# High-part products first, and four gate tiles inside the last attention steps, in a hybrid decoder step

## The chip, the cores and the metric

One core of a Trainium2 chip runs the whole layer. The metric is the device time of one execution in microseconds; before the change the median of three executions is 2021.8 us (2020.32 to 2022.55).

## The reference

One decoder layer (width 2048) is applied to 288 tokens: 32 of eight decode requests, 256 of a prompt. All matrix products use shared float32 weights:

```
xn   = rmsnorm(x)
proj = xn @ w_in            # r, k, v, three small low-rank inputs, q, k, v of attention, gate_a, gate_b
y_a  = rwkv_branch(...)     # token shift, decay, delta-rule state scan, group norm, output gate
y_b  = swa(q, k, v)         # window attention, ALiBi, sinks
mix  = sigmoid(gate_a) * y_a + sigmoid(gate_b) * y_b
h    = x + mix @ w_out
h    = h + relu(rmsnorm(h) @ w_up)^2 @ w_down
y    = rmsnorm(h)
```

Caches and states are returned as well.

## The kernel before

Activations lie transposed: a channel tile has 128 partitions and 288 token columns. Every float32 operand of a large product is split into a high part (rounded to fp32r) and a low part (the rest), and the product is the sum of three: high weight by high activation, high by low, low by high.

**A half tile.** Weights arrive as half tiles of 128 x 1024 (eight blocks of the contraction). `weights` (L152) issues the load of one on SP's queue (L158, four buffers `raw`), ScalarE casts it to `whi` (L146) and VectorE subtracts to get `wlo` (L147); `whi` and `wlo` have two buffers each. `dense` (L164) takes two half tiles for one output tile (one for a half of the output projection). For each of the eight blocks k it issues three matmuls in a row: L177 (`whi`, high activation), L178 (`whi`, low activation), L179 (`wlo`, high activation). So the third matmul of a half tile already needs `wlo`. A dense call accumulates into one of two PSUM banks `mm`; the bank comes free when its result is read out.

**Phase 1** first makes four small tiles while x arrives (L296 to L316; the same three products, L314 to L316, for four tiles and two blocks at a time in four PSUM banks). Then a loop goes over 16 channel tiles (`pair`: k, v and r tiles and their scan operands). Between its parts run steps of the attention generator (`attention`, by a pacing list) and of the side generators: `chain` (the state scan of two channel tiles) and `finish` (output gate, gate tile `ga`, merge, store to `mixd` in DRAM). After the loop come the remaining attention steps, which are the twelve of its last group, each followed by `advance`, three side steps (L403, L404). Then the attention's SBUF pools are closed (L405, L406), and in their place come `h`, `mhi`, `mlo` (L409 to L412) and a pool `late`. The first eight merged tiles are loaded back from DRAM to `h` (L414) and split (L416); the last four gate tiles (channel tiles 12 to 15, `ga12` to `ga15`) are computed (L422) and their tanh is kept in the tiles `tgl` of the pool `late` (L424). The output projection's first half follows (L430, 16 half tiles on `mhi`/`mlo`), then in phase 2 its second half and the MLP, all by `dense`.

**What sets the order.** The program is traced in this order, and a planner then orders each engine's instructions by a simulated timeline; an instruction that is ready may be put ahead of earlier ones that are not. On the chip each engine and SP's queue take their instructions in the planned order. A tile in reused SBUF waits for the last reader of what lay there before.

Of the kernel before, what the change touches and what calls it, by code (L numbers as in the profile page):

```python
# [8 lines left out]
F32 = mybir.dt.float32  # L9
F32R = mybir.dt.float32r  # L10
AF = mybir.ActivationFunctionType
# [6 lines left out]
KT = D // 128  # L18
# [111 lines left out]
class Builder:  # L130
# [33 lines left out]
    def dense(self, src, x, kts=range(KT), pre=None, m=128):  # L164


        nc = self.nc
        ps = self.ps_mm.tile([128, 512], F32, name="mm")
        if m < 128:
            nc.vector.memset(ps[m:128, :NT], 0.0)  # L170
        for i, kt in enumerate(kts):
            if i % 8 == 0:
                whi, wlo = pre[i // 8] if pre else self.weights(src[i // 8])
            k = i % 8
            a, b = whi[:, k * 128:k * 128 + m], wlo[:, k * 128:k * 128 + m]
            hi, lo = x(kt)
            nc.tensor.matmul(ps[:m, :NT], lhsT=a, rhs=hi, start=(i == 0), stop=False)  # L177
            nc.tensor.matmul(ps[:m, :NT], lhsT=a, rhs=lo, start=False, stop=False)  # L178
            nc.tensor.matmul(ps[:m, :NT], lhsT=b, rhs=hi, start=False, stop=(i == len(kts) - 1))  # L179
        return ps[:, :NT]  # L180

    def xin(self, kt):
# [60 lines left out]
    def phase1(self, c1, ph):  # L243
# [16 lines left out]
        with ExitStack() as st:  # L260
            xp = self.pool("xin", 1, ctx=st)
            x = xp.tile([128, KT, NT], F32, name="x")
            shi = xp.tile([128, KT, NT], F32R, name="shi")
            slo = xp.tile([128, KT, NT], F32R, name="slo")
            rstd = xp.tile([128, NT], F32, name="rstd")
            acc = xp.tile([128, 2, NT], F32, name="acc")
            pss = self.ps_lo.tile([128, 512], F32, name="lo")

            win4 = io["win"][TIX["dw"]:TIX["dw"] + 4].rearrange("t a p (k c) -> a p t k c", k=8)
            pz = [pool.tile([128, 512], F32, name=n)[:, :NT] for pool, n in ((self.ps_gr, "gr"), (self.ps_gr, "gr"), (self.ps_ch, "ch"), (self.ps_ch, "ch"))]  # L270

            def arrive(q):
                two = slice(2 * q, 2 * q + 2)
                for kt in (2 * q, 2 * q + 1):
                    w = v["norm_mix_w"][:, kt:kt + 1]
                    if kt % 2:
                        nc.vector.tensor_scalar(out=shi[:, kt, :], in0=x[:, kt, :], scalar1=w, scalar2=None, op0=ALU.mult)
                    else:
                        nc.scalar.activation(out=shi[:, kt, :], in_=x[:, kt, :], func=AF.Copy, scale=w)
                    nc.vector.scalar_tensor_tensor(out=slo[:, kt, :], in0=x[:, kt, :], scalar=w, in1=shi[:, kt, :], op0=ALU.mult, op1=ALU.subtract)  # L280

                sq = acc if q == 2 else xp.tile([128, 2, NT], F32, name="xsq", bufs=2)
                nc.scalar.activation(out=sq, in_=x[:, two, :], func=AF.Square)
                if q < 2:
                    for i in range(2):
                        nc.tensor.matmul(pss[:, :NT], lhsT=self.ones, rhs=sq[:, i, :], start=(q == 0 and i == 0), stop=False)
                elif q > 2:
                    nc.vector.tensor_tensor(out=acc, in0=acc, in1=sq, op=ALU.add)

            def fetch(q):  # L290
                nc.sync.dma_start(out=x[:, 2 * q:2 * q + 2, :], in_=io["xT"][:, 2 * q:2 * q + 2, :])

            AHEAD = 2
            for q in range(AHEAD):
                fetch(q)
            for q in range(8):  # L296
                k2 = 2 * (q % 4)
                raw = self.wraw[0].tile([128, 4, 2, 128], F32, name="raw")
                nc.sync.dma_start(out=raw, in_=win4[q // 4, :, :, k2:k2 + 2, :])
                if q + AHEAD < 8:  # L300
                    fetch(q + AHEAD)
                if q == 0:
                    for i in range(AHEAD):
                        arrive(i)
                elif q + AHEAD - 1 < 8:
                    arrive(q + AHEAD - 1)
                whi = self.whi[0].tile([128, 4, 2, 128], F32R, name="whi")
                wlo = self.wlo[0].tile([128, 4, 2, 128], F32R, name="wlo")
                self.split(whi, wlo, raw)
                for t in range(4):  # L310
                    for k in range(2):
                        kt = 2 * q + k
                        a, b, hi, lo = whi[:, t, k], wlo[:, t, k], shi[:, kt, :], slo[:, kt, :]
                        nc.tensor.matmul(pz[t], lhsT=a, rhs=hi, start=(kt == 0), stop=False)  # L314
                        nc.tensor.matmul(pz[t], lhsT=a, rhs=lo, start=False, stop=False)
                        nc.tensor.matmul(pz[t], lhsT=b, rhs=hi, start=False, stop=(kt == KT - 1))  # L316
                if q == 7 - AHEAD + 1:
                    for i in range(2):
                        nc.tensor.matmul(pss[:, :NT], lhsT=self.ones, rhs=acc[:, i, :], start=False, stop=(i == 1))
                    self.rstd(pss[:, :NT], rstd)  # L320
                if q == 3:
                    nc.sync.dma_start(out=self.ss, in_=io["ss"])
            self.load(self.cst, io["const"])
            nc.vector.tensor_scalar(out=self.omu, in0=self.mu, scalar1=-1.0, scalar2=1.0, op0=ALU.mult, op1=ALU.add)

            def rescale(kts):
                for kt in kts:
                    w = v["norm_mix_w"][:, kt:kt + 1]
                    if kt % 2:
                        nc.vector.scalar_tensor_tensor(out=x[:, kt, :], in0=x[:, kt, :], scalar=w, in1=rstd, op0=ALU.mult, op1=ALU.mult)  # L330
                        self.split(self.xhi[:, kt, :], self.xlo[:, kt, :], x[:, kt, :])
                    else:
                        nc.gpsimd.tensor_tensor(out=x[:, kt, :], in0=x[:, kt, :], in1=rstd, op=ALU.mult)
                        self.split(self.xhi[:, kt, :], self.xlo[:, kt, :], x[:, kt, :], scale=w)

            rescale(range(12))
            for i, n in enumerate(("dw", "da", "dg0", "dg1")):
                z = self.shift(pz[i], n, "rx", rstd)
                if i == 0:
                    nc.scalar.activation(out=z, in_=z, func=AF.Tanh)  # L340
                    rescale(range(12, KT))
                elif i > 1:
                    nc.scalar.activation(out=z, in_=z, func=AF.Tanh, scale=0.5)
                    nc.vector.tensor_scalar(out=z, in0=z, scalar1=0.5, scalar2=0.5, op0=ALU.mult, op1=ALU.add)
                self.split(self.lhi[:, i, :], self.llo[:, i, :], z)
# [54 lines left out]
                flat = lambda t: t.rearrange("t b d -> (t b d)").rearrange("(a c) -> a c", a=16)  # L400
                self.load(flat(io["o_vws"][ct - 1]), flat(io["cv"][ct - 1, TS:W]))
        nc.sync.dma_start(out=io["o_shift"], in_=self.ss)
        for _ in att:  # L403
            self.advance(side, SIDE_STEPS)  # L404
        atc.close()  # L405
        ewc.close()  # L406

# [4 lines left out]
        self.mlo = xm.tile([128, 8, NT], F32R, name="mlo")  # L412
        for q in range(0, 8, 2):
            nc.sync.dma_start(out=self.h[:, q:q + 2, :], in_=self.mixd[q:q + 2].rearrange("c p t -> p c t"))  # L414
        for ct in range(8):
            self.split(self.mhi[:, ct, :], self.mlo[:, ct, :], self.h[:, ct, :], scale=0.5)  # L416
        for q in range(8, KT, 2):
            nc.sync.dma_start(out=self.h[:, q:q + 2, :], in_=io["xT"][:, q:q + 2, :])
        self.late = self.pool("late", 1, ctx=ph, side="right")
        self.tga = {}  # L420
        for ct in range(LATE, KT):
            ps = self.dense(io["win"][TIX[f"ga{ct}"]], self.xin)  # L422
            self.tga[ct] = self.late.tile([128, NT], F32, name="tgl", bufs=KT - LATE)
            nc.scalar.activation(out=self.tga[ct], in_=ps, func=AF.Tanh, scale=0.5)  # L424
            self.advance(side, SIDE_STEPS)
        self.att_done = 4
        for q in range(0, 8, 2):
            nc.sync.dma_start(out=self.h[:, q:q + 2, :], in_=io["xT"][:, q:q + 2, :])
# [427 lines left out]
    def finish(self, G, last):  # L856

        nc, io, fin = self.nc, self.io, self.fin
        for p in range(GP):
            ct = G.g * GP + p  # L860
            hi, lo = self.lora_weights(io["lora2"][ct], "lg", fin)
            if last:
                ta = self.tga[ct]
            else:
                ps = self.dense(io["win"][TIX[f"ga{ct}"]], self.xin)
                ta = fin.tile([128, NT], F32, name="tga", bufs=2)
                nc.scalar.activation(out=ta, in_=ps, func=AF.Tanh, scale=0.5)
            yield 0
            w = lambda i: slice(i * 128, (i + 1) * 128)
# [14 lines left out]
    def attention(self, g):  # L884
# [8 lines left out]
        nc.sync.dma_start(out=sb.rearrange("p a b -> p (a b)"), in_=io["sbias"][g])  # L893
        yield 0
        ps = self.dense(win[TIX[f"av{g}"]], self.xin)
        vs = at.tile([128, NT], F32, name="vs")
        nc.scalar.copy(out=vs, in_=ps)
        tr = self.ps_gr.tile([128, 512], F32, name="gr")
        for c in range(2):
# [309 lines left out]
```

## Time and profile before

| | us |
|---|---|
| median of three executions | 2021.8 |
| the profiled execution | 2020.54 |
| its span (first to last instruction) | 2018.6 |
| TensorE busy | 1939.0 (96%) |
| VectorE busy | 1292.7 (64%) |
| ScalarE busy | 975.8 (48%) |
| mean granted TensorE clock | 0.988 |

The profile counts a matmul as busy until its modelled end, and matmuls overlap in the array, so a busy TensorE may still take them at a slower pace; idle times and start-to-start distances say more. Names: PE is TensorE's matmul, PEld its weight load, DVE VectorE, ACT ScalarE, POOL GpSimd, SP the queue that issues the transfers.

### The profile page before, as it was taken

What the parts mean: (1) busy time and instruction counts of PE and PEld (TensorE: products, weight loads), DVE (VectorE), ACT (ScalarE), POOL (GpSimd) and SP (SyncE); (2) the same over time, 40 slices, a digit from 0 to 9 for tenths busy, and PEclk for the clock granted to TensorE, in tenths of its full rate; (3) what the DMA queues carried; (4) which work ended last, traced back from release to release, by engine and by line L of the source; (5) the groups of instructions that cost most, each with busy time, mean ns of one, the idle gap of its engine ahead of it and who ended that gap; (6) DMA issues with size and microseconds to landing.
All of it is one profiled execution on the core that took longest, in us unless ns stands there. A gap on an engine that the chain in (4) does not pass through costs nothing.

```text
span 2018.6 us, 39509 instructions
## 1 busy us (share of the span) xinstructions
PE 1939.0 (96%) x15470; PEld 1870.5 (93%) x15470; DVE 1292.7 (64%) x2618; ACT 975.8 (48%) x2021; POOL 239.3 (12%) x421
## 2 busy tenths in 40 slices
PE   7999999999999998899989999999999999999997
PEld 6998998989899898888888999999999999999997
DVE  8667777687885867876856675444444454445554
ACT  5655545555454554545544454433543354334443
POOL 3201113121220312313012000000000000000000
PEclk9999999999999999999989999999999999999998
DMA  6444455354543544544446545554545555455452
GB/s 221 153 158 155 141 160 168 121 156 133 185 142 128 159 144 132 164 135 156 123 138 230 178 161 166 168 167 166 164 163 166 166 167 165 165 164 166 163 171 99
DMA packets 160170, 319.30 MB, mean 158 GB/s; under 512 B 58576, under 2 KB 85200, under 8 KB 159920
## 3 DMA queue, kind: packets, MB, share of 16 engines
q1 hardware_dynamic: 159984, 316.77, 49.3%
q8 instruction: 122, 2.00, 0.4%
q14 instruction: 64, 0.52, 0.1%
HBM read 300.22 MB, written 18.52 MB: 158 GB/s over the span
## 4 chain that ended last, share of the span: by engine, by line
PE 57%; DVE 4%; DMA 2%; ACT 1%; issue 1%; POOL 1%; SPq 0%; DVEq 0%; ACTq 0%; POOLq 0%
PE mm L179 18%; PE mm L177 18%; PE mm L178 17%; DVE wlo L147 1%; DMA ybr<-mixd 1%; PE gr L632 0%; DVE utmp L693 0%; DMA raw<-win 0%; PE lo L966 0%; DVE A L695 0%; DMA o_wkvs<-S 0%; DMA S<-wkv 0%; PE gr L938 0%; PE ch L784 0%; DMA h<-mixd 0%
## 5 line engine op out<-in xcount | busy, mean ns | idle before, releaser
L147 DVE TENSOR_TENSOR wlo<-raw,whi 128x1024 fp32r<-128x1024 f32 x504 | 623.5, 1238 | 428.8 <-ACT whi L146 425.5
L146 ACT CAST whi<-raw 128x1024 fp32r<-128x1024 f32 x504 | 527.5, 1048 | 624.0 <-PE mm L178 570.9
L179 PE MATMUL mm<-xhi,wlo 128*128 128x288 f32 x2304 | 698.5, 303 | 24.6 <-DVE wlo L147 24.5
L177 PE MATMUL mm<-xhi,whi 128*128 128x288 f32 x2304 | 691.8, 300 | 4.2 <-ACT ks L890 2.3
L178 PE MATMUL mm<-xlo,whi 128*128 128x288 f32 x2304 | 689.0, 299 | 0.0
L179 PEld LDWEIGHTS mm<-xhi,wlo 128*128 128x128 f32 x2304 | 435.8, 189 | 38.0 <-DVE wlo L147 32.3
L177 PEld LDWEIGHTS mm<-xhi,whi 128*128 128x128 f32 x2304 | 435.5, 189 | 11.2 <-issue 3.6
L178 PEld LDWEIGHTS mm<-xlo,whi 128*128 128x128 f32 x2304 | 435.4, 189 | 3.7 <-issue 1.7
L177 PE MATMUL mm<-uh,whi 128*128 128x288 f32 x1024 | 302.4, 296 | 0.0
L179 PE MATMUL mm<-uh,wlo 128*128 128x288 f32 x1024 | 301.5, 295 | 0.0
L178 PE MATMUL mm<-ul,whi 128*128 128x288 f32 x1024 | 300.8, 294 | 0.0
L178 PEld LDWEIGHTS mm<-ul,whi 128*128 128x128 f32 x1024 | 192.9, 188 | 0.0
L179 PEld LDWEIGHTS mm<-uh,wlo 128*128 128x128 f32 x1024 | 192.6, 188 | 0.0
L177 PEld LDWEIGHTS mm<-uh,whi 128*128 128x128 f32 x1024 | 192.1, 188 | 0.0
L179 PE MATMUL mm<-mhi,wlo 128*128 128x288 f32 x640 | 190.1, 297 | 1.6 <-DVE wlo L147 1.5
L178 PE MATMUL mm<-mlo,whi 128*128 128x288 f32 x640 | 189.3, 296 | 0.0
L177 PE MATMUL mm<-mhi,whi 128*128 128x288 f32 x640 | 188.4, 294 | 0.0
L179 PEld LDWEIGHTS mm<-mhi,wlo 128*128 128x128 f32 x640 | 120.3, 188 | 2.8 <-DVE wlo L147 2.3
L177 PEld LDWEIGHTS mm<-mhi,whi 128*128 128x128 f32 x640 | 120.2, 188 | 0.4 <-issue 0.2
L178 PEld LDWEIGHTS mm<-mlo,whi 128*128 128x128 f32 x640 | 120.4, 188 | 0.2 <-issue 0.2
L1101 POOL TENSOR_TENSOR h<-h,rstd 128x288 f32<-128x288 f32 x5 | 3.8, 796 | 910.1 <-ACT rstd L1097 910.1
L693 DVE TENSOR_TENSOR utmp<-A,U 108x84 f32<-108x84 f32 (+12 forms) x240 | 67.3, 281 | 34.0 <-DMA A<-scr 24.7
(333 smaller groups left out, 2260.5 us busy)
## 6 DMA issues: line engine op xcount, KB each, us to landing
raw<-win SPq DMA_DIRECT2D x216, 512.0 KB
raw<-wup SPq DMA_DIRECT2D x128, 512.0 KB
raw<-wdn SPq DMA_DIRECT2D x128, 512.0 KB
raw<-wout SPq DMA_DIRECT2D x32, 512.0 KB
S<-wkv SPq DMA_DIRECT2D x32, 256.0 KB
lraw<-lora SPq DMA_DIRECT2D x32, 128.0 KB
o_wkvs<-S SPq DMA_DIRECT2D x16, 256.0 KB
U<-scr SPq DMA_DIRECT2D x24, 144.0 KB
```

Of the source, the lines that this page charges most:

```text
L146: nc.scalar.copy(out=dst_hi, in_=src)
L147: nc.vector.tensor_tensor(out=dst_lo, in0=src, in1=dst_hi, op=ALU.subtract)
L177: nc.tensor.matmul(ps[:m, :NT], lhsT=a, rhs=hi, start=(i == 0), stop=False)
L178: nc.tensor.matmul(ps[:m, :NT], lhsT=a, rhs=lo, start=False, stop=False)
L179: nc.tensor.matmul(ps[:m, :NT], lhsT=b, rhs=hi, start=False, stop=(i == len(kts) - 1))
L693: nc.vector.tensor_tensor(out=tv, in0=A[:, 0:n, j:j + 1].broadcast_to([3 * NU, n, m]), in1=U[:, j:j + 1, j + 1:32].broadcast_to([3 * NU, n ...
L1101: nc.gpsimd.tensor_tensor(out=h[:, ct, :], in0=h[:, ct, :], in1=rstd, op=ALU.mult)
```

## The change

In `dense` the half tile's products are issued in two passes: for all eight blocks the two products with `whi`, then for all eight the product with `wlo`. The four tiles at the start get the same in three passes. The gate tiles `ga12` and `ga13` are now traced after the tenth and eleventh of the last twelve attention steps, each with three side steps behind it; `ga14` and `ga15` are traced after the attention's pools are closed, each ahead of four of the eight splits of the merged tiles. Their tanh goes to the pool `fin` (tile `tga`, now four buffers, shared with `finish`); the pool `late` is gone. The attention's value tile `vs` now shares the buffer of the gate tile `tg`.

```diff
-        for i, kt in enumerate(kts):
-            if i % 8 == 0:
-                whi, wlo = pre[i // 8] if pre else self.weights(src[i // 8])
...
-            nc.tensor.matmul(ps[:m, :NT], lhsT=a, rhs=hi, start=(i == 0), stop=False)
-            nc.tensor.matmul(ps[:m, :NT], lhsT=a, rhs=lo, start=False, stop=False)
-            nc.tensor.matmul(ps[:m, :NT], lhsT=b, rhs=hi, start=False, stop=(i == len(kts) - 1))
+        for i in range(0, len(kts), 8):
+            whi, wlo = pre[i // 8] if pre else self.weights(src[i // 8])
+            for k in range(8):
+                a = whi[:, k * 128:k * 128 + m]
+                hi, lo = x(kts[i + k])
+                nc.tensor.matmul(ps[:m, :NT], lhsT=a, rhs=hi, start=(i + k == 0), stop=False)
+                nc.tensor.matmul(ps[:m, :NT], lhsT=a, rhs=lo, start=False, stop=False)
+            for k in range(8):
+                nc.tensor.matmul(ps[:m, :NT], lhsT=wlo[:, k * 128:k * 128 + m], rhs=x(kts[i + k])[0],
+                                 start=False, stop=(i + k == len(kts) - 1))
...
-                for t in range(4):
-                    for k in range(2):
...
+                steps = [(t, k, 2 * q + k) for t in range(4) for k in range(2)]
+                for w, part in ((whi, shi), (whi, slo), (wlo, shi)):
+                    for t, k, kt in steps:
+                        nc.tensor.matmul(pz[t], lhsT=w[:, t, k], rhs=part[:, kt, :], start=(kt == 0 and part is shi and w is whi),
+                                         stop=(kt == KT - 1 and w is wlo))
...
-        for _ in att:
+        self.tga = {}
+        def gate(ct):
+            ps = self.dense(io["win"][TIX[f"ga{ct}"]], self.xin)
+            self.tga[ct] = self.fin.tile([128, NT], F32, name="tga", bufs=KT - LATE)
+            nc.scalar.activation(out=self.tga[ct], in_=ps, func=AF.Tanh, scale=0.5)
             self.advance(side, SIDE_STEPS)
+        late = iter(range(LATE, KT))
+        for n, _ in enumerate(att):
+            self.advance(side, SIDE_STEPS)
+            if n >= 9 and n < 11:
+                gate(next(late))
         atc.close()
         ewc.close()
...
-        for ct in range(8):
-            self.split(self.mhi[:, ct, :], self.mlo[:, ct, :], self.h[:, ct, :], scale=0.5)
+        for half, ct in enumerate(late):
+            gate(ct)
+            for i in range(half * 4, half * 4 + 4):
+                self.split(self.mhi[:, i, :], self.mlo[:, i, :], self.h[:, i, :], scale=0.5)
...
-        self.late = self.pool("late", 1, ctx=ph, side="right")
-        self.tga = {}
-        for ct in range(LATE, KT):
-            ps = self.dense(io["win"][TIX[f"ga{ct}"]], self.xin)
-            self.tga[ct] = self.late.tile([128, NT], F32, name="tgl", bufs=KT - LATE)
-            nc.scalar.activation(out=self.tga[ct], in_=ps, func=AF.Tanh, scale=0.5)
-            self.advance(side, SIDE_STEPS)
...
-                ta = fin.tile([128, NT], F32, name="tga", bufs=2)
+                ta = fin.tile([128, NT], F32, name="tga", bufs=KT - LATE)
...
-        vs = at.tile([128, NT], F32, name="vs")
+        vs = at.tile([128, NT], F32, name="vs", tag="tg", bufs=1)
```

## Rows read from the trace of the kernel before

**Rows 1.** The page: TensorE's busy share and granted clock, 40 slices, in tenths

```profile
PE   7999999999999998899989999999999999999997
...
PEclk9999999999999999999989999999999999999998
```

**Rows 2.** Windows by stage: stretch, us, busy us (instructions) by engine, clock, DMA share, GB/s

```profile
46.90:1042.60 995.70, 950.64 (x8048) 889.47 (x8048) 752.23 (x1892) 527.75 (x1372) 208.92 (x365) 0.99 0.49 148
1042.60:1064.20 21.60, 15.24 (x152) 13.00 (x152) 8.22 (x29) 5.71 (x18) 0.00 (x0) 0.62 0.30 87
...
1136.70:2003.70 867.00, 867.00 (x6532) 866.81 (x6530) 439.05 (x541) 377.99 (x526) 0.00 (x0) 1.00 0.50 163
```

**Rows 3.** Waits of TensorE, 46.5 to 1042 us: total us, times, longest us

```profile
PE mm L179 <- DVE wlo L147: 24.2, 26, 3.7
PE lo L198 <- DVE ysb L1023: 3.1, 3, 1.5
```

**Rows 4.** Timeline of TensorE: start us, us, instruction [idle before]

```profile
186.04 0.40 PE L179 MATMUL mm<-xhi,wlo 128*128 128x288 f32 x1 [2.62 <-DVE wlo L147]
...
317.12 0.40 PE L179 MATMUL mm<-xhi,wlo 128*128 128x288 f32 x1 [3.69 <-DVE wlo L147]
...
317.74 0.44 PE L179 MATMUL mm<-xhi,wlo 128*128 128x288 f32 x1
317.98 0.44 PE L177 MATMUL mm<-xhi,whi 128*128 128x288 f32 x1
...
868.54 0.40 PE L179 MATMUL mm<-xhi,wlo 128*128 128x288 f32 x1 [1.54 <-DVE wlo L147]
...
1100.40 0.40 PE L179 MATMUL mm<-mhi,wlo 128*128 128x288 f32 x1 [0.73 <-DVE wlo L147]
```

**Rows 5.** Timeline of VectorE ahead of 317.12

```profile
313.77 0.69 DVE L851 TENSOR_TENSOR S<-ch,S 128x512 f32<-128x512 f32 x1 [5.01 <-DMA S<-wkv]
...
315.07 2.00 DVE L147 TENSOR_TENSOR wlo<-raw,whi 128x1024 fp32r<-128x1024 f32 x1
```

**Rows 6.** Timeline at the start: TensorE and ScalarE

```profile
33.80 0.43 PE L316 MATMUL gr<-shi,wlo 128*128 128x288 f32 x2
34.07 0.29 PE L314 MATMUL gr<-shi,whi 128*128 128x288 f32 x1
...
36.47 0.29 PE L315 MATMUL ch<-slo,whi 128*128 128x288 f32 x1
41.40 0.61 PE L316 MATMUL gr<-shi,wlo 128*128 128x288 f32 x1 [4.64 <-DVE wlo L147]
...
46.90 0.40 PE L179 MATMUL mm<-xhi,wlo 128*128 128x288 f32 x1 [1.50 <-DVE wlo L147]
...
45.04 1.05 ACT L146 CAST whi<-raw 128x1024 fp32r<-128x1024 f32 x1 [3.02 <-PE ch L315]
```

**Rows 7.** Timeline of TensorE and ScalarE after the attention

```profile
1064.19 0.44 PE L177 MATMUL mm<-xhi,whi 128*128 128x288 f32 x1
...
1079.72 0.29 PE L177 MATMUL mm<-mhi,whi 128*128 128x288 f32 x1
...
1063.05 0.70 ACT L424 ACTIVATE tgl<-mm 128x288 f32<-128x288 f32 x2
1065.89 1.61 ACT L149 ACTIVATE mhi<-h 128x288 fp32r<-128x288 f32 x4 [2.14 <-DMA h<-mixd]
```

**Rows 8.** Matmuls of L177 on `xhi`, 1020 to 1090 us: count, ns, first and last start

```profile
L177 PE MATMUL mm<-xhi,whi x68: 288/295/442, 1019.9 to 1078.8; 128*128 128x288 f32 x68
```

**Rows 9.** VectorE after the attention: last low splits, first output-projection result

```profile
1070.87 0.82 DVE L150 SCALAR_TENSOR_TENSOR mlo<-h,mhi 128x288 fp32r<-128x288 f32 x2
...
1084.24 0.46 DVE L431 TENSOR_TENSOR h<-h,mm 128x288 f32<-128x288 f32 x1 [1.28 <-PE mm L179]
```

**Rows 10.** SP's queue, 1020 to 1150 us: waits of the weight loads; the issue of `vp`

```profile
SPq L158 <- DVE wlo L147: 52.6, 23, 4.3
...
1047.55 7.43 SPq L1015 DMA_DIRECT2D vp<-cv x2
```

More of the change, by code (lines that the diff above doesn't have):

```diff
@@ L170, in dense @@
             nc.vector.memset(ps[m:128, :NT], 0.0)
-        for i, kt in enumerate(kts):
-            if i % 8 == 0:
-                whi, wlo = pre[i // 8] if pre else self.weights(src[i // 8])
-            k = i % 8
-            a, b = whi[:, k * 128:k * 128 + m], wlo[:, k * 128:k * 128 + m]
-            hi, lo = x(kt)
-            nc.tensor.matmul(ps[:m, :NT], lhsT=a, rhs=hi, start=(i == 0), stop=False)
-            nc.tensor.matmul(ps[:m, :NT], lhsT=a, rhs=lo, start=False, stop=False)
-            nc.tensor.matmul(ps[:m, :NT], lhsT=b, rhs=hi, start=False, stop=(i == len(kts) - 1))
+        for i in range(0, len(kts), 8):
[8 more added lines that the diff above has]
+                                 start=False, stop=(i + k == len(kts) - 1))
         return ps[:, :NT]
@@ L309, in phase1 @@
                 self.split(whi, wlo, raw)
-                for t in range(4):
-                    for k in range(2):
[L312 to L316, printed above, removed]
+                steps = [(t, k, 2 * q + k) for t in range(4) for k in range(2)]
[3 more added lines that the diff above has]
+                                         stop=(kt == KT - 1 and w is wlo))
                 if q == 7 - AHEAD + 1:
```

## The prediction

> **What bounds the kernel now.** I read the page first: TensorE is busy in nearly every one of the forty slices, at nearly full clock [rows 1]. The windows by stage then divide the span. From 1136.7 to 2003.7 us TensorE has no idle time: 6532 matmuls in 867.0 us, and 6528 of them are dense (272 half tiles of 24), which makes one each 867.0/6528 = 0.1328 us [rows 2]. Nothing waits there, so a new order within a half tile can change it only if the pace itself changes. What there is to win lies ahead: from 46.9 to 1042.6 us TensorE is idle for 995.7 - 950.6 = 45.1 us, and from 1042.6 to 1064.2 us it is busy for 15.2 of 21.6 us at a granted clock of 0.62, a mean of its two levels (1.2 and 2.4 GHz) [rows 2]. The view of TensorE's waits names the first: 24.2 of the 45.1 us are L179 waiting for `wlo`, in 26 places, and no other single wait has more than 3.1 us [rows 3]. The timelines name the second, below.
>
> VectorE is busy for 752 of these 995.7 us, 76% [rows 2]. So it is late now and then, not too slow on the whole; I take the waits for delays that a longer lead absorbs.
>
> **Part 1: high products first, in the dense tiles.** Today two products of a half tile can run before `wlo` is needed; with the change sixteen can. The lead grows by 14 products, 14 x 0.1328 = 1.86 us. No instruction is added: the same loads, casts, subtractions and matmuls. `whi` comes free after 16 products in place of 23, so the next cast may start earlier; `wlo` comes free with the last product as before.
>
> Of the 26 waits, one (1.50 us at 46.90) belongs to the start, below. The other 25 sum to 22.7 us. Two are longer than 1.86 us, 3.69 and 2.62 us [rows 4]; of them (3.69 - 1.86) + (2.62 - 1.86) = 2.6 us stays. So at most 20.1 us goes. A wait also costs a slow restart: behind 317.12 products start 317.98 - 317.74 = 0.24 us apart in place of 0.13 [rows 4], the clock's half level. I count one such step for each wait, 25 x 0.1 = 2.5 us. Upper bound 22.6 us; lower bound nothing, if VectorE's order merely moves. I take three quarters, 17.0 us: the third-longest wait is 1.54 us [rows 4], and the 23 without the two long ones have a mean of (22.7 - 6.3)/23 = 0.71 us, which the lead covers whole.
>
> What holds `wlo` is the work ahead of it on VectorE. At 317.12 TensorE waits because `wlo` stood behind an addition that had itself waited 5.01 us for a transfer of the state [rows 5]; such a head of the queue delays everything behind it. The Trainium skill, page "PSUM — Partial Sum Buffer", section "Engine vs sequencer instructions", states that ScalarE's and VectorE's queues are strictly first in, first out. Taken alone it would say that a late `wlo` stays late and that only the lead is won, 20.1 us and not 22.7 us; the trace agrees with its 5.01 us, and the sum above already goes by the row.
>
> Where these stalls go, the next lateness shows: the waits for attention results and for state transfers (45.1 - 24.2 = 20.9 us in the same stretch). TensorE arrives there earlier, and the planner orders all engines anew. I put a loss of a fifth of it on that, 4 us; bounds 0 and 10 us (half of it more).
>
> **Part 2: the four tiles at the start.** The planner already runs eight high products ahead of `wlo` (36.47 is the last), then TensorE idles 4.64 us until 41.40, and the first dense tile waits 1.50 us at 46.90 [rows 6]. After the change sixteen run ahead, and the next cast of `whi`, which waited 3.02 us for L315 [rows 6], can come before 45.0. VectorE still makes its low parts one after the other here, so I count only the eight products that move ahead of the wait (1.06 us) and the 1.50 us: 2.5 us; bounds 0 and 6.1 (both waits).
>
> **Part 3: the gate tiles.** L177 runs 68 times on `xhi` after 1019.9 us [rows 8]: four gate tiles of 16 and the last 4 of the tile before. So `ga12` and `ga13` already run before 1042.6 though they are traced later. Then both `mm` banks are full: their tanh writes `tgl`, which lies where the attention's tiles lay, and comes only at 1063.05 [rows 7]. Until then no dense product can start; TensorE has only the chain's and the attention's small matmuls. `ga14` and `ga15` (96 products, 96 x 0.1328 = 12.7 us) run from 1064.19, and the output projection begins at 1079.72 [rows 7].
>
> With `tga` in the pool `fin` the tanh of `ga12` can follow its last product and the bank comes free. `ga14` and `ga15` need only `xhi`, weights and a bank, so I expect the planner to put them into the stretch from 1042.6. It holds 6.4 us of plain idle time, and the rest of its work would run at full clock; 12.7 us of products just fit. What is late next is `mhi`: its splits wait for `h` and start at 1065.89 [rows 7], and the last `mlo` ends at 1070.87 + 0.82 = 1071.7 [rows 9]. The first half tile of the projection then ends no sooner than 1071.7 plus its eight `wlo` products, 1072.8; its result was read at 1084.24 [rows 9]. Gain at most 11.4 us. The dense products stand between the small matmuls of the attention's last, latency-bound steps and delay them; I allow 2.5 us. So 9 us; bounds 0 (the chain stretches by as much as is filled) and 12.7.
>
> The gates' eight weight loads issue on SP's queue among the loads of `vp`, whose two issues hold it for 7.43 us from 1047.55 [rows 10]; four of them now fall here. I cost them at nothing, since the raw buffers run ahead; without that cover each costs up to the 4.3 us of the longest such wait [rows 10].
>
> **The rest.** In the projection's first half two waits of 0.73 us go (one is in [rows 4]): 1.5 us. `vs` in `tg`'s buffer: the previous group's `tg` was read four attention steps earlier, so nothing; bound by the longest wait of TensorE for an attention result, 1.5 us [rows 3], in three groups, 4.5 us. Two more `tga` buffers cost nothing.
>
> **Sum**, against the profiled execution's 2020.5 us (span 2018.6 and 1.9 around it; 1.3 us below the median): 17.0 + 2.5 + 9 + 1.5 - 4 = 26.0 us less, 1994.5 us, and with the median's 1.3 us more, 1996. All upper bounds together, 22.6 + 6.1 + 12.7 + 1.5 = 42.9 us, would leave 1979; a third of the gains, 10 us, 2012.
>
> **Rivals.**
> - *VectorE takes over.* Its 76% may hide stretches near its limit; there a lead of 1.86 us is used up once and the waits come back. For it: its queue was held for 5.01 us, longer than the lead [rows 5]. Against it: all but two of the waits are shorter than the lead [rows 4]. Half of parts 1 and 2 is lost: 1996 + 10 = 2006. Chance 0.15.
> - *The gates don't fill the gap*, because the attention's last steps stretch or the planner keeps `ga14` and `ga15` behind them. For it: that chain is latency-bound, with a clock of 0.62 [rows 2]. Against it: `ga12` and `ga13` were already pulled forward. 1996 + 9 = 2005. Chance 0.14.
> - *Slower: SP's queue.* A gate's weight load that waits for a free `raw` stands ahead of the loads of `vp` and `h`, and each holds the queue for up to 4.3 us [rows 10]. Eight such make 34 us, on the path to `mhi`; the other parts save 17 + 2.5 + 1.5 - 4 = 17 us, so it would be 2021.8 - 17 + 34 = 2039. It decides from 17 us of stretch, four loads at the longest wait. Against it: only four loads move and the weights run four buffers ahead. Chance 0.08.
> - *The products change pace.* 11,904 dense products: 1 ns each is 11.9 us, either way. The start shows `wlo` products directly behind each other at (34.07 - 33.80)/2 = 0.135 us [rows 6], the usual pace, so I see no reason; 0.02. The Trainium skill, page "TensorE: Matmul & The Clock Gate", section "Back-to-back issue gap", gives 288/2.4 + 2.5 = 122.5 ns for an isolated one; an estimate by that page would take 10 ns off each, some 120 us, and no stretch here shows that pace.
> - *It does not do what it says*: the planner restores the old order, as it hoisted products at the start. Then parts 1 and 2 fall away: 2021.8 - 9 = 2013. Chance 0.03.
>
> **The numbers.** The forecast has 0.58, with 1981 to 2004 as its own range. The range that holds 8 in 10 reaches over the first two rivals and to the bound of all gains: 1979 to 2012. A change under 0.2% (4 us) could not be told from none. Slower 0.08 (SP's queue 0.07 of its 0.08, pace 0.01), same 0.05 (remnants of the rivals), faster 0.87.
>
> **What would show it.** Right: L179's waits for `wlo` before 1042 us under 8 us in the new trace; the tanh of the four gates right behind their products; no stretch near the attention's end at a clock of 0.62; `h` read at the first projection result some 9 us less behind the attention's last step; the stretch after it still 867 us. Wrong: waits for `wlo` above 15 us, or new waits of TensorE for attention tiles, state loads or `whi` of the same sum; SP's queue blocked by weight loads ahead of `vp` or `h`; a pace other than 0.133 us.

## The result, and the profile after

The median falls from 2021.8 to 1998.18 us (three runs, 1996.91 to 2003.3): a ratio of 0.9882 [0.9854, 0.9911]. The prediction, 1996.0 in a range of 1979 to 2012, was right in sign and close in size. Two of its terms were not: the start cost time where it was to gain, and the pace moved.

The page of the changed kernel, TensorE's busy share and clock in 40 slices; the slices that are 8 in [rows 1] are 9 now, and the first has fallen from 7 to 6:

```profile
PE   6999999999999999999999999999999999999997
...
PEclk9999999999999999999999999999999999999998
```

Its windows by stage (columns as in [rows 2]): the stretch up to about where the gap began before, from there to the first product of the output projection, and the stretch without idle time:

```profile
47.40:1025.70 978.30, 944.19 (x7983) 887.48 (x7983) 758.15 (x1895) 533.07 (x1374) 208.26 (x364) 0.99 0.49 149
1025.70:1059.30 33.60, 30.33 (x335) 27.75 (x334) 19.37 (x48) 12.87 (x29) 0.99 (x2) 0.98 0.53 168
1117.00:1986.80 869.80, 869.79 (x6532) 869.45 (x6530) 430.64 (x541) 385.10 (x525) 0.00 (x0) 1.00 0.50 162
```

Three things are to be seen. The idle time of the first stretch is 978.3 - 944.2 = 34.1 us, against 45.1 in [rows 2]. The gap's clock of 0.62 is gone. And the same 6532 matmuls at the end now take 869.8 us in place of 867.0.

TensorE's waits, 47 to 1042 us (us in total, times, longest), to be held against [rows 3]:

```profile
PE mm L178 <- DVE xlo L150: 8.2, 1, 8.2
PE lo L563 <- ACT ta L554: 3.3, 3, 1.6
PE lo L193 <- DVE A L702: 2.9, 1, 2.9
PE lo L1024 <- DMA vp<-cv: 2.9, 2, 1.6
```

No wait for `wlo` is left (24.2 us before). A new one of 8.2 us heads the list; it belongs to the start. The timeline there, first TensorE, then VectorE (L319 is the sum-of-squares matmul that gives `rstd`, L208 the end of `rstd`, L330 and L150 what is scaled by it and split):

```profile
33.00 1.13 PE L319 MATMUL lo<-acc,ones 128*128 128x288 f32 x4
38.81 0.40 PE L177 MATMUL mm<-xhi,whi 128*128 128x288 f32 x1 [1.49 <-ACT xhi L149]
47.37 0.61 PE L178 MATMUL mm<-xlo,whi 128*128 128x288 f32 x1 [8.16 <-DVE xlo L150]
47.77 0.44 PE L177 MATMUL mm<-xhi,whi 128*128 128x288 f32 x1
...
35.36 1.95 DVE L208 RECIPROCAL rstd<-rstd 128x288 f32<-128x288 f32 x1 [0.51 <-ACT rstd L207]
39.19 5.86 DVE L330 SCALAR_TENSOR_TENSOR x<-x,vec,rstd 128x288 f32<-128x288 f32 x6
46.81 0.50 DVE L150 SCALAR_TENSOR_TENSOR xlo<-x,vec,xhi 128x288 fp32r<-128x288 f32 x1
```

The same places before the change (the reciprocal is L206 there):

```profile
26.04 1.13 PE L319 MATMUL lo<-acc,ones 128*128 128x288 f32 x4
...
45.10 0.29 PE L178 MATMUL mm<-xlo,whi 128*128 128x288 f32 x1
...
28.24 1.95 DVE L206 RECIPROCAL rstd<-rstd 128x288 f32<-128x288 f32 x1 [0.51 <-ACT rstd L205]
```

The waits of 4.64 and 1.50 us in [rows 6] are gone, but the sum-of-squares matmul and the reciprocal come 7 us later, and the first product on `xlo` comes 2.3 us later.

The end of the attention, first ScalarE (`pP` is the copy ahead of the last attention product, `tga` the four late gates), then the projection's first product and first result, then the window between these two:

```profile
1022.20 0.42 ACT L409 ACTIVATE tga<-mm 128x288 f32<-128x288 f32 x1
1033.31 0.41 ACT L409 ACTIVATE tga<-mm 128x288 f32<-128x288 f32 x1
1039.05 0.37 ACT L1015 COPY pP<-gr 128x256 f32<-128x256 f32 x1 [1.97 <-PE gr L1012]
1041.48 0.41 ACT L409 ACTIVATE tga<-mm 128x288 f32<-128x288 f32 x1
1052.19 0.41 ACT L409 ACTIVATE tga<-mm 128x288 f32<-128x288 f32 x1
...
1059.27 0.85 PE L177 MATMUL mm<-mhi,whi 128*128 128x288 f32 x2 [2.98 <-ACT mhi L149]
...
1067.27 0.45 DVE L438 TENSOR_TENSOR h<-h,mm 128x288 f32<-128x288 f32 x1 [2.67 <-PE mm L180]
...
1059.27:1067.27 8.00, 8.00 (x41) 8.00 (x42) 4.98 (x12) 5.53 (x11) 3.63 (x5) 0.65 1.02 380
```

The last `pP` before the change:

```profile
1051.14 0.37 ACT L1008 COPY pP<-gr 128x256 f32<-128x256 f32 x1 [0.94 <-PE gr L1005]
```

The tanh of each gate follows its products, and the projection begins at 1059.27 in place of 1079.72 [rows 7]. From five such marks in each profiled execution the span can be cut, and the cuts of two kernels subtracted. The marks are the first read of a dense tile (`ks`), the last `pP`, the first product on `mhi`, the first product of the projection's second half, and the last product:

```
us            to ks   ks to pP   pP to mhi   projection,   last      time of
                                             first half    stretch   this execution
before        62.70   988.44     28.58       56.99         867.14    2020.54
after         63.37   975.68     20.22       57.71         869.82    2003.30
dense_only    60.99   971.30     29.43       54.41         869.82    2002.79
gates_only    61.74   998.11     19.80       66.10         867.14    2029.53
no_start      59.77   969.26     19.98       56.82         869.82    1991.60
lead4         59.44   979.60     17.45       62.43         868.49    2004.26
pool_only     59.81   967.60     18.76       57.69         869.9     1990.29
vs_share      62.80   995.35     28.68       57.48         867.14    2027.79
pool_old      65.19  1000.82     19.23       61.32         867.1     2030.07
stat_early    57.88   966.13     20.22       57.39         869.82    1987.47
```

For after against before: +0.7 - 12.8 - 8.4 + 0.7 + 2.7 = -17.1 us, all but 0.1 us of the difference of these two executions (2003.3 is the longest of its three). Two cautions: each row is one execution, and `pP` is no clean border, since dense products can move across it. 96 of them lie between `pP` and `mhi` before the change and 64 after it; the 32 others (4.2 us) now stand in the stretch ahead. The rest of this text says where the five terms come from.

### The profile page after: what moved, and what is told of

Its sections match the earlier page's. It is cut to its first block, busy times and chain, and to the rows that moved or that the text cites. A ratio compares the mean times of both kernels' runs of the same rounds, so it can differ in the third digit from the quotient of the medians.

```text
span 2001.5 us, 39526 instructions
## 1 busy us (share of the span) xinstructions
PE 1935.0 (97%) x15470; PEld 1872.6 (94%) x15470; DVE 1289.4 (64%) x2618; ACT 988.5 (49%) x2019; POOL 238.6 (12%) x421
## 4 chain that ended last, share of the span: by engine, by line
PE 56%; DVE 5%; DMA 2%; ACT 1%; issue 1%; POOL 0%; SPq 0%; DVEq 0%; ACTq 0%; POOLq 0%
PE mm L177 18%; PE mm L178 18%; PE mm L180 17%; DVE wlo L147 1%; DVE A L702 0%; DVE utmp L700 0%; PE gr L639 0%; ACT whi L146 0%; PE gr L945 0%; PE lo L973 0%; PE ch L801 0%; DMA o_wkvs<-S 0%; PE ch L791 0%; DMA h<-mixd 0%; PE ch L808 0%
## 5 line engine op out<-in xcount | busy, mean ns | idle before, releaser
L178 PE MATMUL mm<-xlo,whi 128*128 128x288 f32 x2304 | 644.6, 302 | 8.2 <-DVE xlo L150 8.2
L177 PE MATMUL mm<-xhi,whi 128*128 128x288 f32 x2304 | 645.0, 303 | 4.8 <-ACT whi L146 2.3
L177 PEld LDWEIGHTS mm<-xhi,whi 128*128 128x128 f32 x2304 | 437.8, 190 | 11.9 <-issue 3.6
L180 PE MATMUL mm<-xhi,wlo 128*128 128x288 f32 x2304 | 374.2, 299 | 0.0
L180 PEld LDWEIGHTS mm<-xhi,wlo 128*128 128x128 f32 x2304 | 326.9, 189 | 3.8 <-issue 2.6
L177 PE MATMUL mm<-uh,whi 128*128 128x288 f32 x1024 | 275.8, 297 | 0.0
L177 PEld LDWEIGHTS mm<-uh,whi 128*128 128x128 f32 x1024 | 192.6, 188 | 0.0
L177 PE MATMUL mm<-mhi,whi 128*128 128x288 f32 x640 | 175.1, 299 | 3.0 <-ACT mhi L149 3.0
L180 PE MATMUL mm<-uh,wlo 128*128 128x288 f32 x1024 | 157.0, 296 | 0.0
L180 PEld LDWEIGHTS mm<-uh,wlo 128*128 128x128 f32 x1024 | 143.0, 188 | 0.0
L177 PEld LDWEIGHTS mm<-mhi,whi 128*128 128x128 f32 x640 | 121.8, 191 | 3.5 <-ACT mhi L149 3.2
L1080 DVE TENSOR_TENSOR h<-h,mm 128x288 f32<-128x288 f32 x64 | 29.1, 455 | 130.8 <-PE mm L180 130.8
L180 PE MATMUL mm<-mhi,wlo 128*128 128x288 f32 x640 | 97.8, 295 | 0.0
L180 PEld LDWEIGHTS mm<-mhi,wlo 128*128 128x128 f32 x640 | 89.0, 188 | 0.0
```

Source lines behind the costliest of these rows:

```text
L177: nc.tensor.matmul(ps[:m, :NT], lhsT=a, rhs=hi, start=(i + k == 0), stop=False)
L180: nc.tensor.matmul(ps[:m, :NT], lhsT=wlo[:, k * 128:k * 128 + m], rhs=x(kts[i + k])[0], start=False, stop=(i + k == len(kts) - 1))
L1080: nc.vector.tensor_tensor(out=h[:, ct, :], in0=h[:, ct, :], in1=ps, op=ALU.add)
```

## The experiments

Each was compared with 9 to 23 executions of the kernel before on the same chip, whose median was 2022 to 2023 us. The first four below ran on one chip, the next four on a second, the last four on a third, and of the changed kernel there are only the three executions above; from group to group it is the ratios that compare.

**The dense order alone** (`dense_only`): the first hunk of the diff, nothing else.

> Only the order of the products in the dense tiles is the new one; the start and the gate tiles are as before. Lead theory: TensorE's waits for wlo between 47 and 1042 us fall from 24 us to under 3 us, other waits take back a third to a half, and the run is 8 to 14 us faster than before. Pace theory (the new order itself makes each product a little slower): the stretch of the output projection's second half and the MLP takes 869.8 us as in the changed kernel, not 867.0. Rival to both (the pace differs from execution to execution): 867.0 here. Rival to the lead theory (all gain is in the gates): within 3 us of before.

Measured: 2002.47 us, 0.9894 [0.9878, 0.991]. No wait for `wlo` from 46.5 to 1030 us, and the gap stays as it was. Its window over the gap, and then ScalarE's timeline with the last `pP` and the gates' first tanh:

```profile
1030.00:1045.00 15.00, 12.45 (x93) 10.71 (x94) 4.27 (x18) 3.03 (x10) 0.00 (x0) 0.51 0.17 48
```

```profile
1032.29 0.37 ACT L1009 COPY pP<-gr 128x256 f32<-128x256 f32 x1 [0.94 <-PE gr L1006]
1044.10 0.70 ACT L425 ACTIVATE tgl<-mm 128x288 f32<-128x288 f32 x2
```

At 0.51 nearly the whole stretch ran at the lower of the two clock levels, with 93 matmuls. This part carries most of the gain by itself: 20.7 us, against a median of 2023.18 us before. The expectation of 8 to 14 us was too low.

**The gates' part alone** (`gates_only`): the change, with the old order of products in `dense` and at the start.

> Only the gate tiles' part: traced between the last attention steps, tanh to the pool fin, vs in tg's buffer; products in the old order. Theory: the two full banks come free, ga14 and ga15 run before the attention's end, the clock there stays near 1.0, and the run is 7 to 11 us faster than before; waits for wlo stay near 24 us, and the last stretch stays at 867.0 us. Rival (the gates only gain because wlo comes earlier): under 3 us faster.

Measured: 2029.32 us, 1.0031 [1.0018, 1.0044]: slower, against the gain that was expected. Yet the gap is filled: 19.8 us from `pP` to `mhi` in place of 28.6. Its windows, from `pP` to `mhi` and the projection's first half, and that half in the kernel before:

```profile
1059.85:1079.65 19.80, 16.99 (x191) 15.17 (x189) 10.25 (x28) 7.47 (x17) 0.80 (x1) 1.00 0.50 160
1079.65:1145.75 66.10, 61.09 (x409) 58.12 (x409) 40.64 (x62) 26.30 (x39) 13.03 (x13) 0.92 0.60 198
...
1079.72:1136.71 56.99, 55.38 (x407) 53.61 (x405) 35.40 (x47) 22.94 (x30) 9.00 (x11) 1.00 0.57 185
```

The 8.8 us won behind `pP` are no net gain. 42 dense products (5.6 us) moved ahead of `pP`, and by the table `ks` to `pP` is 9.7 us longer, so that `ks` to `mhi` takes 1017.9 us against 1017.0 before. Part of this is clock: its mean is 0.985 in this execution and 0.988 in that of the kernel before. The projection's first half adds 9.1 us, with more idle time and a clock of 0.92. On SP's queue the two loads of `vp` also stand 12 us apart, with weight loads between them:

```profile
1052.37 0.33 SPq L1023 DMA_DIRECT2D vp<-cv  x1
1054.75 8.74 SPq L158 DMA_DIRECT2D raw<-wout  x3
1064.19 0.33 SPq L1023 DMA_DIRECT2D vp<-cv  x1
```

That is the picture of the prediction's slower rival, but by itself it shows no cost; `pool_old` below bears on it.

**The start alone** (`start_only`): the second hunk of the diff.

> Only the four tiles at the start in the new order. Prediction's step: 2.5 us faster, since eight more products run ahead of wlo. Rival, from the changed kernel's trace: the matmul of the norm's sum of squares comes at 33 us in place of 26 behind the products of more pairs, rstd and the split of x come some 7 us later on VectorE, and the run is 0 to 4 us slower than before.

Measured: 2026.8 us, 1.0016 [1.0, 1.0032], slower if anything, as the rival has it. The late `rstd` is there again; TensorE's rows:

```profile
34.08 1.13 PE L317 MATMUL lo<-acc,ones 128*128 128x288 f32 x4
...
48.45 0.61 PE L178 MATMUL mm<-xlo,whi 128*128 128x288 f32 x1 [8.17 <-DVE xlo L150]
```

**The change without its start** (`no_start`): the second hunk undone.

> The changed kernel with the old order at the start. If the start's new order costs what its trace suggests, 1 to 4 us faster than the changed kernel (1994 to 1997 in place of 1998), and the norm's matmul stands near 26 us again. If the start's order gains 2.5 us as predicted, 2001. Parts that add up: dense alone plus gates alone within 4 us of this run's gain; a gain below the larger of the two would speak for a planner that reorders at random.

Measured: 1992.61 us, 0.9852 [0.9832, 0.9872], 5.6 us below the changed kernel's median, though the intervals of the two ratios overlap (0.9882 [0.9854, 0.9911]). `ks` is read at 59.77 us in place of 63.37. Against `dense_only` (0.9894) the gates' part is now worth some 9 us, and the same edit was worth minus 6 with the old order. The expectation had the two parts add up within 4 us. They do not: alone they give 20.7 and -6.1 us, together 30.6. The second gains only with the first; why was not settled.

**The sum of squares ahead of the sixth round** (`stat_early`), on the changed kernel:

```diff
-                elif q + AHEAD - 1 < 8:
+                elif q + AHEAD - 1 < 7:
...
+                if q == 5:
+                    arrive(7)
+                    for i in range(2):
+                        nc.tensor.matmul(pss[:, :NT], lhsT=self.ones, rhs=acc[:, i, :], start=False, stop=(i == 1))
+                    self.rstd(pss[:, :NT], rstd)
...
-                if q == 7 - AHEAD + 1:
...
```

> The changed kernel, with the arrival of the last two channel tiles and the sum-of-squares matmul traced before the sixth round of start products instead of after the seventh. Theory A (the start lost because the planner no longer hoists that matmul, so rstd and everything rescaled by it come late): the matmul at 26 to 27 us in place of 33.0, the first product on xlo some 14.4 us behind it, at about 41 in place of 47.37, the first read of a dense tile near 57 in place of 63.37, and the time 5 to 6.5 us below the changed kernel, near 1992. Rival B (the start is bound by its 192 products and the low splits behind them): the matmul moves, the first xlo product stays within 1.5 us of 47.37, no gain.

Measured: 1987.5 us, 0.9831 [0.9817, 0.9845]. Theory A holds for the start. TensorE's rows:

```profile
26.94 1.13 PE L312 MATMUL lo<-acc,ones 128*128 128x288 f32 x4
40.40 0.61 PE L178 MATMUL mm<-xlo,whi 128*128 128x288 f32 x1 [3.41 <-DVE xlo L150]
```

The matmul stands 6.06 us earlier than in the changed kernel, the first product on `xlo` 6.97 us, `ks` 5.5 us. So at the start of the changed kernel the chain through `rstd` decides. The new order seems to help there too, once that matmul is not left behind it: against `no_start` the matmul stands later (26.94 and 25.58 us), yet the first product on `xlo` comes earlier (40.40 and 45.20 us). The whole time fell by 10.7 us where 5 to 6.5 were expected. In the table 9.6 us of the difference to the changed kernel lie between `ks` and `pP`, behind the start, and what they come from is open.

**The old order in phase 2 alone** (`old_phase2`), on `no_start`: `dense` takes the old loop once phase 2 has begun.

> The changed kernel with the old start, and in phase 2 alone the old order of products. Theory A (the order itself sets the pace): the stretch from the first x product behind the projection's first half to the last u product goes back from 869.82 to 867.14 us, the whole to 2.7 us below the kernel with the old start (1992.6), 1990. Rival B (the pace hangs on something else that differs, such as where the stretch starts): 869.8 stays, 1992.6.

Measured: 1987.41 us, 0.9832 [0.9816, 0.9847]. The last stretch:

```profile
1104.93:1972.07 867.14, 867.14 (x6532) 866.80 (x6530) 438.77 (x541) 375.78 (x525) 0.00 (x0) 1.00 0.47 162
```

The pace goes back with the order, to the hundredth: the order sets it. (The time fell by 5.2 us and not by 2.7; the rest is within the spread of the runs.)

**Groups of four blocks** (`lead4`), on `no_start`:

```diff
-            for k in range(8):
-                a = whi[:, k * 128:k * 128 + m]
+            for g in (0, 4):
+              for k in range(g, g + 4):
+                a = whi[:, k * 128:k * 128 + m]
...
-            for k in range(8):
+              for k in range(g, g + 4):
```

> The changed kernel with the old start, and the two passes over groups of four blocks: eight high products, four low, eight high, four low. The lead is 6 products longer than before the change, 0.80 us, in place of 1.86. Theory A (the waits are delays that a lead absorbs, each by its length): of the 25 waits of the kernel before 7.8 us stick out over 0.80 us against 2.6 over 1.86, so about 5 us slower than the kernel with the old start (1992.6), near 1998; the waits for wlo come back at 3 to 8 us in a few places. Rival B (what counts is that two products precede no longer decides; any lead does): no wait for wlo and 1992 to 1993. Rival C (only the full group lets whi free early enough): over 2005.

Measured: 2004.79 us, 0.9915 [0.99, 0.993], 12 us above `no_start`. The waits came back as theory A has it. TensorE's waits from 46.5 to 1030 us, and the window of the last stretch:

```profile
PE mm L181 <- DVE wlo L147: 6.5, 8, 2.2
```

```profile
1118.92:1987.41 868.49, 868.49 (x6530) 868.15 (x6530) 438.10 (x542) 378.58 (x525) 0.00 (x0) 1.00 0.47 162
```

That is 6.5 us in 8 places, within the 3 to 8 us expected. But the time is twice theory A's loss: by the table 10.3 us go from `ks` to `pP` and 5.6 us in the projection's first half, and 4 come back elsewhere. Rival C's time, over 2005, was missed by 0.2 us only, and ScalarE's waits for a free `whi` did grow, from 129.1 us in `no_start` to 181.6 (46.5 to 1030 us). Against it, `dense_only` has 162.8 us of these and no wait for `wlo`. So the shorter lead and the later release of `whi` are not told apart. The pace is halfway, 868.49.

**Only the tanh's place** (`pool_only`), on `no_start`: the four gates are traced where they were, behind the eight splits; their tanh stays in `fin`.

> The new order in dense, the old start, and the tanh of the four late gates in the pool fin, but the four gate tiles traced at their old place, behind the eight splits. Theory A (the old tanh tiles, which had to wait for the attention's memory, held the two mm banks; once they don't, the planner fills the gap by itself): tanh of the gates behind their products, before 1045 us, no stretch at clock 0.5 between 1030 and 1045, the time near 1993. Rival B (the traced place decides): the second pair of gates still comes after the attention's end, time near the 2002.5 us of the dense part alone. Rival C (half and half): the first pair's tanh early, the second pair early too, but the splits of h behind them, 1996 to 2000.

Measured: 1989.98 us, 0.9843 [0.9827, 0.9859], level with `no_start`. ScalarE's rows:

```profile
1010.77 0.42 ACT L411 ACTIVATE tga<-mm 128x288 f32<-128x288 f32 x1
1023.10 0.38 ACT L411 ACTIVATE tga<-mm 128x288 f32<-128x288 f32 x1
1027.41 0.37 ACT L1015 COPY pP<-gr 128x256 f32<-128x256 f32 x1 [0.24 <-PE gr L1012]
```

Theory A holds: the planner fills the gap by itself once a tanh can leave its bank. The code that moves the gates between the attention steps is not what gains.

**The shared buffer alone** (`vs_share`): the kernel before, with the last line of the diff.

> The kernel before with one edit alone: the attention's value tile shares the buffer of the gate tile. Theory A (it costs nothing, as the prediction had it): within 2 us of the kernel before. Rival B (it is what made the gates' part slower with the old order: the value tile waits for the last reader of the gate tile, and the last group's attention falls behind): 4 to 7 us slower, and the three last attention score copies later than before by as much.

Measured: 2023.94 us, 1.0002 [0.9987, 1.0016]: nothing, as the prediction had it. (The score copies of its profiled execution are late, as rival B has it, but that execution is one of the longer of twelve, 2017.8 to 2030.1 us, at a mean clock of 0.984; over the twelve nothing is lost.)

**Only the tanh's place, old order** (`pool_old`): `pool_only` with the old products everywhere.

> The kernel before with the gates' tanh in the pool fin and the value tile in the gate tile's buffer, the four gate tiles traced at their old place and the old order of products everywhere. Theory A (where the gates are traced cost 6 us with the old order, by weight loads between the vp loads; the freed banks themselves gain): tanh of the gates by 1045 to 1055 us, the time 5 to 9 us below the kernel before, as pool_only against the dense part alone (12 us) less its calmer neighbours. Rival B (with the old order the attention's last steps have no room for two more gate tiles, wherever they are traced): 2026 to 2031, like gates_only. Rival C (without the traced place the planner leaves the second pair behind): within 3 us of the kernel before.

Measured: 2023.38 us, 1.0008 [0.9995, 1.0021]: no gain, no loss. Theory C's time came, though not by its mechanism: the gap is filled (19.2 us from `pP` to `mhi`). The profiled execution is the longest of its twelve; `vs_share`, whose profiled execution has the same mean clock of 0.984, is the nearer one to hold it against. By the table this one is 9.5 us shorter from `pP` to `mhi` and 5.5 us longer from `ks` to `pP`, where 42 more dense products (5.6 us) stand; the projection's first half takes 3.8 us more and the start 2.4. The 5 to 6 us between this and `gates_only` may be what the traced place costs with the old order; the two intervals just touch, so I hold that loosely, and whether it is the `vp` loads stays open.

**Early start and old phase 2 together** (`both`), and **that with the tanh's place alone** (`both_pool`):

> The changed kernel with the early sum-of-squares matmul and the old order of products in phase 2. Theory A (the two effects lie in different stretches and add): phase 2 at 867.14 us, 2.7 us below stat_early (1987.5), 1985. Rival B (the early start's gain was a luckier order of phase 1, which any edit shuffles again): above 1989.

> As both, with the four gate tiles traced at their old place and only their tanh in the pool fin. Theory A (the freed banks are all of the gates' gain, the traced place none of it): within 3 us of both, 1982 to 1988. Rival B (the traced place is worth something once the start is early): 4 us or more above both.

Measured: 1989.03 us, 0.9837 [0.9821, 0.9853], and 1987.74 us, 0.9827 [0.981, 0.9844]. For `both` the last stretch is back near the old pace (867.49 us; 868.03 in `both_pool`), but the time lies at the edge of rival B; what the pace saves is within the spread of the rest, and the two theories are not told apart. `both_pool` is level with `both`, as theory A says. The best four kernels lie from 1987.4 to 1989.0 us and these runs do not tell them apart. By the ratios all are some 10 us faster than the changed kernel.

## Why the prediction was right, and where not

**Part 1, the dense order: right, by its mechanism.** Predicted 17.0 us won and 4 given back; in the table the stretch from `ks` to `pP` is 12.8 us shorter after the change, although 4.2 us of the gates' products moved into it. Alone, in `dense_only`, this part gave more than forecast: 20.7 us, against 17.0 - 4 + 1.5 = 14.5 with the projection's waits. All of the 24.2 us of waits went, the two that were longer than the lead too. The prediction kept 2.6 us of those. The Trainium skill (page "PSUM — Partial Sum Buffer", section "Engine vs sequencer instructions") calls VectorE's queue strictly first in, first out. A queue in the old order would then have kept them, but the planner also ordered VectorE's work anew. The addition that had waited 5.01 us at 313.77 [rows 5] now comes behind a transposition and waits 1.06 us:

```profile
309.85 0.69 DVE L858 TENSOR_TENSOR S<-ch,S 128x512 f32<-128x512 f32 x1 [1.06 <-DMA S<-wkv]
```

`lead4` shows that groups of eight blocks do better than groups of four; that it is the lead, and not the earlier release of `whi`, is argued.

**The planner's loss of 4 us: the term was too small.** Its base was too: the 24.2 us that it takes off hold the wait of 1.50 us that ends at 46.90 us, where its stretch begins, so the other waits were 45.1 - 22.7 = 22.4 us and not 20.9. In `no_start`, from 46.5 to 1013 us, TensorE's idle time is 29.4 us (966.50 - 937.13): 7.0 us came back, within the bounds of 0 to 10. In the changed kernel 34.1 - 22.4 = 11.7 us came back, outside them. Part 1 made up for it, since the waits for `wlo` went whole. Why the late start leaves 4.7 us more of it was not settled.

**Part 2, the start: wrong in sign.** The step that failed is "I count only the eight products that move ahead of the wait (1.06 us) and the 1.50 us". It priced the waits of [rows 6] and did not ask what else the planner had put into that stretch. The two waits did go. But L319, traced behind the seventh of eight rounds, had stood at 26.04 us, with 18.8 us of products and waits behind it, up to 44.84; in the new order it stands at 33.00, with one round behind it, and `rstd` and all that is scaled by it wait for it. The other runs agree: `ks` is 66.58 - 62.70 = 3.9 us later with this edit alone (`start_only`), 3.6 earlier when it is undone (`no_start`), 5.5 earlier with the matmul traced early (`stat_early`). This mark also moves from execution to execution (61.74 to 65.19 us with the old start and the old order), so the first product on `xlo` is the steadier sign: 44.69 to 46.40 us in the nine runs with the old start, 47.37 and 48.45 with the new one, 40.40 to 40.98 in the three with the early matmul. That the planner pulled it forward because the old order left TensorE idle in its simulated timeline is argued, not tried.

**Part 3, the gates: right in size, not in reason.** Predicted 9 us; from `pP` to `mhi` 8.4 us went, half of which are products moved ahead of `pP` (into what had been idle time there). The cleaner measure is `no_start` against `dense_only`, 9.9 us by their medians on one chip. By the prediction's own sign it is less: the first projection result comes 28.2 us behind `pP` in place of 33.1, since the first half tile now starts behind a wait of 2.98 us for `mhi` and runs at a clock of 0.65. The prediction named both reasons, the bank and the place in the trace; `pool_only` shows that the bank is enough. That the gain depends on part 1 was not foreseen: with the old order the gap was filled too, and nothing was won. In `gates_only` the projection's first half grew by 9.1 us: TensorE is idle for 5.0 us there (1.6 before), and a clock of 0.92 costs some 5.3 of its 66.1 us. What stretches it in this way is open.

**The projection's 1.5 us** did not show: 57.7 us in place of 57.0. Its two waits for `wlo` are gone, but at a clock of 0.65 its first 8.00 us lost 0.35 x 8.00 = 2.8 us, and the prediction had not reckoned with that.

**The pace: small, and not foreseen.** 869.82 - 867.14 = 2.7 us over 6528 products, 0.41 ns each. The prediction saw "no reason" from the start's spacing of 0.135 us, which is too coarse to show this. By the Trainium skill's formula for an isolated matmul (page "TensorE: Matmul & The Clock Gate", section "Back-to-back issue gap") 122.5 ns would be the estimate. Neither order met it: 132.8 and 133.2 ns.

**The rivals.** VectorE did not take over: no wait for `wlo` came back at the full lead. The gap was filled. SP's queue did not decide: in `pool_only`, too, the `vp` loads stand 10 us apart (1021.25 and 1031.51), and it is among the fastest. The planner restored the old order nowhere. Against this execution the sum of 26.0 us missed by 8.9: the start 3.2, the pace 2.7, the projection 2.2, the gates 0.6, the dense part 0.2. The median missed by only 2.2 us because it lies 5.1 us below this execution. That closeness is in part luck. By the medians of `dense_only`, `no_start` and the changed kernel the dense order gave 20.7 us (14.5 forecast), the gates on top of it 9.9 (9), and the start took back some 5.6 (2.5 to be gained): errors of opposite sign.

## What to carry to other kernels

Where a late operand stalls an engine for a short time, putting the work that does not need it first can remove the stall; here 24.2 us of waits were worth 20.7 us. A stall that a planner may have filled with something else is not free to remove: look at what stands in it, above all at the head of a chain that others wait for, and trace that explicitly early. And a buffer that is reused too soon can hold up an engine two steps away; freeing it may do all that a rewritten order was meant to do.

## What the runs showed that was not expected

**The spread between executions goes largely with TensorE's clock.** Twelve executions of `vs_share` go from 2017.80 us at a mean granted clock of 0.990 to 2030.14 us at 0.983; 0.007 of some 2025 us is 14 us, about the 12.3 us between them (in between the order is not strict: 2018.16 us came at 0.986). Where I looked, the loss falls in short stretches behind a wait of TensorE, but not behind every one. In the kernel before, the stretches behind the waits of 2.62 us (186.04) and 3.69 us (317.12) [rows 4] differ:

```profile
186.00:192.00 6.00, 5.96 (x45) 5.96 (x46) 5.92 (x15) 2.58 (x8) 1.94 (x3) 1.00 0.54 179
316.00:322.00 6.00, 4.88 (x37) 4.46 (x37) 5.59 (x10) 3.58 (x9) 4.71 (x7) 0.72 0.66 172
```

The second lost 0.28 x 6 = 1.7 us. So the prediction's 0.1 us of slow restart for each wait was far too little for some and too much for others. An estimate of the loss over all executions of a kernel, time x (1 - mean clock), is 30.5 to 30.8 us for the kernel before on the three chips, 27.2 for `vs_share`, 21.6 for `dense_only`, 17.9 for `no_start`, 15.4 for `stat_early` and 20.5 for `lead4`. So of the 20.7 us that `dense_only` gained some 30.5 - 21.6 = 8.9 are clock, where the prediction had 2.5. That fewer waits make for fewer such stretches fits this, but the stretches were not counted.

**The order of products sets the pace by 0.3%.** The last stretch takes 867.14 us with the old order, 868.49 with groups of four and 869.82 with groups of eight. In the changed kernel the eight products on `wlo` keep 1.06 us and the sixteen high ones take 2.14 us:

```profile
1982.37:1983.43 1.06, 1.06 (x10) 1.06 (x9) 0.00 (x0) 0.00 (x0) 0.00 (x0) 1.00 0.00 0
1983.43:1985.57 2.14, 2.14 (x19) 2.14 (x18) 0.00 (x0) 0.00 (x0) 0.00 (x0) 1.00 0.00 0
```

1.06/8 = 0.1325 and 2.14/16 = 0.1338 us. Over the whole stretch the mean distance from one start to the next is 132.4 ns from a `wlo` product to the next one, and 133.1 to 134.0 ns from a high product to the next. So it is the high products that are slower in the new order. Why, was not tried.
